# Gate and up products of two SwiGLU passes by seven products in place of eight, with the down products set between them

## The chip, the cores and the metric

One of the eight NeuronCores of a Trainium2 chip runs the whole program. The metric is the device time of one execution in microseconds (us), lower is better; the median of three runs stands for a kernel.

## The reference, cut to what matters

A decoder layer: a half-step SwiGLU FFN, two mixers side by side (attention and RWKV-7), and a second half-step FFN, over 1040 tokens (16 meta tokens and 1024) with d_model 1024 and d_ff 2816, all in float32.

```python
def swiglu(h, w_gate, w_up, w_down):
    return (jax.nn.silu(h @ w_gate) * (h @ w_up)) @ w_down
...
        n = rms_norm(h, ffn1_norm[l])
        h = h + 0.5 * swiglu(n, ffn1_w_gate[l], ffn1_w_up[l], ffn1_w_down[l])
...
        n = rms_norm(h, ffn2_norm[l])
        h = h + 0.5 * swiglu(n, ffn2_w_gate[l], ffn2_w_up[l], ffn2_w_down[l])
```

## The kernel before

**Tokens.** They go in two groups, A (528, in chunks of 256 and 272) and B (512). The order on TensorE is: ffn1 of A, projections of A, ffn1 of B, projections of B, the output product, ffn2 of A, ffn2 of B; the mixers' work is woven in between. Everything is kept with features on the 128 partitions and tokens along the free axis.

**Three matmuls per product.** A float32 operand is split into two fp32r tiles, a high part (ScalarE, `ACTIVATE`, tiles `whi`, `nh`, `ah`) and the rest (`wlo`, `nl`, `al`: a subtraction on VectorE, for most `al` on GpSimd). `mm3` issues high by high, high by low and low by high into one PSUM bank. Weights are split on the chip too: each 128x1024 block is loaded as `wraw` (512 KB, queue of SP), split into `whi` and `wlo`, and used once.

**One FFN (`ffn`).** The 22 tiles of 128 d_ff columns go in `PARTS` of 2, 4, 4, 4, 4 and 4 tiles. A gate tile is 8 contraction steps of `mm3` over the tokens (`pg`), then a sigmoid and a multiplication into `sl`; an up tile the same into `pu`, then a multiplication and the split into `ah`, `al`. After the tiles of a part (and the next part's first gate) come its down products (`pd`), four blocks `wraw` of 4 x 256 columns, each added into the residual `h` on VectorE. In group A each matmul has 256 or 272 columns; in group B's ffn2 it has 512, with 256 at its start and end.

**Other names.** `groupB(j)` (j = 0 to 3) normalizes and transposes 128 tokens of group B during A's ffn1 and writes them to DRAM (`nbd`, `xbd`); it uses the pool `xp`. `fin0` writes A's final output during the first tiles of B's ffn2, `final` writes B's at the end. `director` opens the mixers' pools after A's ffn1.

**What sets the order.** No order is written out for VectorE, ScalarE, GpSimd and SP: `Clock` records each instruction with a cost, keeps a modelled time for every engine (one shared `port` for GpSimd and those VectorE operations whose inputs all lie in SBUF), and puts the instructions out in the order in which they could start by it, urgent ones first. The result is one fixed program; on the chip each engine goes through its own list in order, waiting on semaphores. All instructions are issued from one recording line, so the profile shows the same line for all, and tiles tell them apart.

## Time and profile before

| what | us |
|---|---|
| runs of before: median of 3 (lowest, highest) | 2320.24 (2317.2, 2322.21) |
| the profiled execution: its time | 2319.39 |
| its span, first to last instruction | 2317.7 |
| PE (TensorE) busy in the span | 2275.8 (98%) |
| DVE (VectorE) busy | 1368.8 (59%) |
| ACT (ScalarE) busy | 965.5 (42%) |
| POOL (GpSimd) busy | 484.7 (21%) |

A row that lists instructions gives engine, operation, output tile <- input tiles and shapes; matmuls are pipelined, so that the time from one start to the next is what one costs, not its busy time. PEclk is the clock that TensorE was granted as a share of 2.4 GHz. A window row gives the window, its length, and for each engine its busy time with the number of instructions.

### The profile page before, as it was taken

The numbers are of one execution on the slowest core, as the hardware profiler recorded it, in microseconds if no ns is written. First come the engines' busy times: TensorE is split into PE (matmuls) and PEld (weight loads), VectorE is DVE, ScalarE is ACT, GpSimd is POOL, SyncE is SP. The second block draws the span as 40 slices with busy tenths as digits, with TensorE's granted clock in tenths as the row PEclk, the third lists the DMA queues.
The fourth block names the chain that finished last, engine by engine and source line by source line (L and its number), as shares of the span: only waits on it lengthen the run. The fifth ranks groups of instructions, "written<-read, shape, count | busy, mean of one in ns | idle before, by whom it ended". The sixth has DMA issues, their size and how long they took to land.

```text
span 2317.7 us, 40064 instructions
## 1 busy us (share of the span) xinstructions
PE 2275.8 (98%) x15931; PEld 1988.3 (86%) x15931; DVE 1368.8 (59%) x2325; ACT 965.5 (42%) x1871; POOL 484.7 (21%) x650
## 2 busy tenths in 40 slices
PE   7999999999999999999999989999999999999998
PEld 7999999999878788778878978887877898888888
DVE  5644444675776655676576877647777566433435
ACT  5422223543444434555434544445666333222222
POOL 0100011012042341441012324313544010000000
PEclk9999999999999999999999989999999999999999
DMA  4632322445652332422556433333222533333332
GB/s 129 191 117 88 91 89 91 139 139 138 213 138 81 93 92 83 119 90 74 159 142 195 137 96 98 91 89 119 82 77 69 154 99 124 91 100 91 91 100 82
DMA packets 412095, 259.59 MB, mean 112 GB/s; under 512 B 45060, under 2 KB 396500, under 8 KB 411908
## 3 DMA queue, kind: packets, MB, share of 16 engines
q1 hardware_dynamic: 411908, 257.04, 37.4%
q8 instruction: 125, 2.05, 0.4%
q14 instruction: 62, 0.51, 0.1%
HBM read 222.99 MB, written 33.99 MB: 111 GB/s over the span
## 4 chain that ended last, share of the span: by engine, by line
PE 93%; DVE 3%; DMA 1%; ACT 1%; issue 1%; POOL 0%; DVEq 0%; SPq 0%; ACTq 0%; POOLq 0%
PE pd L83 33%; PE pu L83 22%; PE pg L83 21%; PE pwo L83 3%; PE px L83 3%; PE po L83 2%; PE pz L83 2%; PE pat L83 2%; DVE wlo L83 1%; PE pG L83 1%; PE psw L83 0%; ACT whi L83 0%; DMA wraw<-in_ffn_w_gate_dram 0%; PE pp L83 0%; PE pxn L83 0%
## 5 line engine op out<-in xcount | busy, mean ns | idle before, releaser
L83 ACT ACTIVATE whi<-wraw 128x1024 fp32r<-128x1024 f32 (+1 forms) x348 | 366.7, 1054 | 528.2 <-PE pd L83 308.7
L83 DVE TENSOR_TENSOR wlo<-wraw,whi 128x1024 fp32r<-128x1024 f32 (+1 forms) x348 | 439.3, 1262 | 107.3 <-ACT whi L83 103.0
L83 PE MATMUL pd<-ah,whi 128*128 128x512 f32 (+2 forms) x944 | 326.1, 345 | 1.3 <-DVE h L83 1.2
L83 PE MATMUL pd<-al,whi 128*128 128x512 f32 (+2 forms) x944 | 318.4, 337 | 0.9 <-DVE al L83 0.8
L83 PE MATMUL pd<-ah,wlo 128*128 128x512 f32 (+2 forms) x944 | 318.9, 338 | 0.0
L83 POOL TENSOR_TENSOR al<-sl,ah 128x512 fp32r<-128x512 f32 (+1 forms) x83 | 124.5, 1500 | 925.4 <-ACT ah L83 925.2
L83 PE MATMUL pu<-nh,whi 128*128 128x512 f32 (+2 forms) x752 | 257.1, 342 | 0.0
L83 PE MATMUL pg<-nh,whi 128*128 128x512 f32 (+2 forms) x736 | 256.5, 348 | 0.0
L83 PE MATMUL pu<-nh,wlo 128*128 128x512 f32 (+2 forms) x752 | 248.0, 330 | 1.5 <-DVE wlo L83 1.5
L83 PE MATMUL pu<-nl,whi 128*128 128x512 f32 (+2 forms) x752 | 247.7, 329 | 0.0
L83 PE MATMUL pg<-nh,wlo 128*128 128x512 f32 (+2 forms) x736 | 246.6, 335 | 0.8 <-DVE wlo L83 0.8
L83 PE MATMUL pg<-nl,whi 128*128 128x512 f32 (+2 forms) x736 | 246.4, 335 | 0.2 <-DVE nl L83 0.2
L83 PE MATMUL pd<-nh,whi 128*128 128x256 f32 (+7 forms) x648 | 210.1, 324 | 0.9 <-DVE st L83 0.8
L83 PE MATMUL pd<-nh,wlo 128*128 128x256 f32 (+7 forms) x648 | 204.3, 315 | 0.4 <-DVE wlo L83 0.4
L83 PE MATMUL pd<-nl,whi 128*128 128x256 f32 (+7 forms) x648 | 204.1, 315 | 0.0
L83 PEld LDWEIGHTS pd<-ah,whi 128*128 128x128 f32 x944 | 177.5, 188 | 23.9 <-issue 2.6
L83 PEld LDWEIGHTS pd<-ah,wlo 128*128 128x128 f32 x944 | 177.7, 188 | 20.5
L83 PEld LDWEIGHTS pd<-al,whi 128*128 128x128 f32 x944 | 177.8, 188 | 19.6 <-DVE al L83 2.0
L83 DVE TENSOR_TENSOR sl<-pg,sl 128x512 f32<-128x512 f32 (+2 forms) x116 | 65.5, 564 | 199.8 <-ACT sl L83 199.5
L83 DVE SCALAR_TENSOR_TENSOR h<-pd,h 128x256 f32<-128x256 f32 (+1 forms) x200 | 107.9, 543 | 91.6 <-PE pd L83 90.4
L83 DVE TENSOR_TENSOR sl<-pu,sl 128x256 f32<-128x256 f32 (+2 forms) x119 | 65.9, 553 | 154.0 <-PE pu L83 153.5
L83 ACT ACTIVATE sl<-pg 128x512 f32<-128x512 f32 (+2 forms) x116 | 57.6, 497 | 234.5 <-PE pg L83 206.0
(275 smaller groups left out, 4826.0 us busy)
## 6 DMA issues: line engine op xcount, KB each, us to landing
wraw<-in_ffn_w_gate_dram SPq DMA_DIRECT2D x92, 512.0 KB
wraw<-in_ffn_w_up_dram SPq DMA_DIRECT2D x92, 512.0 KB
wraw<-in_ffn_w_down_dram SPq DMA_DIRECT2D x88, 512.0 KB
wraw<-in_w_in_dram SPq DMA_DIRECT2D x54, 512.0 KB
wraw<-in_w_out_dram SPq DMA_DIRECT2D x18, 512.0 KB
s<-rkvd SPq DMA_DIRECT2D x18, 256.0 KB
raw<-qkvd SPq DMA_DIRECT2D x16, 264.0 KB
raw<-qkvd SPq DMA_DIRECT2D x16, 256.0 KB
```

The lines of the kernel that those rows point to most:

```text
L83: self._c.trace(self._n, op, lambda: f(*a, **k), out, [x for x in args if isinstance(x, bass.AP)], k)
```

## The change

In the first FFN of group A and the last of group B, the d_ff tiles from 6 on (`QF`) are taken in pairs, for which gate (and up, but for the last pair) is computed as a *quad*: with the contraction halved, the two weight tiles of the pair as the other halving, and the tokens halved (w = 264 in A, 256 in B), the 2 x 2 block product is done with seven block products (Strassen in Winograd's form) instead of eight. A block product is 4 contraction steps of three matmuls over w columns.

- **Weight sums (`pair`).** Of the two raw tiles a1, a2 of a pair GpSimd forms s1, s2, s4, s3 (`qs`, 128x512 each), and five blocks are split into `qh`, `ql` (s1, s2, s4, s3 and half of a2); a1 is split whole into `whi`, `wlo`. The ring of `qh`, `ql` has seven places.
- **Token sums (`sums`).** Once per FFN, t1 to t4 are formed from the normalized tokens (`tt`) and split, four steps k.
- **Results (`quad`).** Partial results stay in PSUM; four copies to `sn` on ScalarE and four additions on VectorE put the two results together in SBUF tiles `cc` (2w wide). The sigmoid and both multiplications then read `cc` from SBUF.
- **Order (`quad_order`).** Down products of one part (d) stand between the quads of the next: d d d d g6 u6 g8 u8 | g10 d u10 d d g12 d u12 | g14 d u14 d d g16 d u16 | and so on; the last up pair is done plainly.
- **Memory.** The quads' pools take the place of `xp` and `wx` in A's ffn1, and of A's `h` and `n` and the pool `f2x` in B's ffn2, and open when `groupB` and `fin0` have let go of them. `groupB(j)` waits for block j - 2 instead of j - 1. The stage pool of the projections opens after the quads. B's `final` takes its output tiles from the ring `cc`.

```diff
+QF = 6
 PARTS = [(0, 2), (2, 6), (6, 10), (10, 14), (14, 18), (18, 22)]
...
+def quad_order():
+    for i, (f0, _) in enumerate(PARTS):
+        if f0 >= QF:
+            q = 0
+            for x in "ddddgu gu" if f0 == QF else "gdudd gdu":
+                if x == " ":
+                    f0 += 2
+                elif x == "d":
+                    yield x, PARTS[i - 1], q
+                    q += 1
+                else:
+                    yield x, None, f0
...
+class Fast:
+    def __init__(self, pools, w):
+        self.p, self.tp, self.q = pools
+        self.w, self.nq, self.nc, self.ns, self.k = w, 7, 7, 4, 0
+        self.t = {i: [self.tp.tile([P, 4, w], F32R, name="t%d%s" % (i, c)) for c in "hl"] for i in (1, 2, 3, 4)}
...
-            yield self.need(bank=(self.wp, "wr", 2))
-            self.wr.append((x, self.wraw(*x[:3])))
-            self.hold(self.wr[-1][1:])
+            raws = []
+            if isinstance(x[0], tuple):
+                for src, ring in zip(x[0], ((self.wp, "wr", 2), (self.fast.q, "wr2", 2))):
+                    yield self.need(bank=ring)
+                    raws.append(self.wraw(src, *x[1:3], ring))
+                    self.hold(raws[-1:])
+            else:
+                yield self.need(bank=(self.wp, "wr", 2))
+                raws.append(self.wraw(*x[:3]))
+                self.hold(raws)
+            self.wr.append((x, raws))
...
+        s1 = yield from part((a2[:, lo4], a2[:, hi4], ALU.add))
+        self.clock.ahead = True
+        self.split(w[0], w[1], a1)
+        out.append(([w[0][:, lo4], w[1][:, lo4]], ()))
+        out.append(([w[0][:, hi4], w[1][:, hi4]], w))
+        self.clock.ahead = False
+        s2 = yield from part((s1[1], a1[:, lo4], ALU.subtract))
+        halves(*s1)
+        a22 = yield from part()
+        self.split(a22[0], a22[1], a2[:, hi4])
+        self.clock.ahead = False
+        s4 = yield from part((a1[:, hi4], s2[1], ALU.subtract))
+        halves(*s2)
+        out.append((a22, a22))
+        s3 = yield from part((a1[:, lo4], a2[:, lo4], ALU.subtract))
+        halves(*s4)
+        halves(*s3)
...
-        half = [[self.fp.tile([P, 4, NA], F32R, tag="n%s%d" % (c, q), name="n%s%d" % (c, q)) for q in range(2)] for c in "hl"]
+        half = [[self.hp.tile([P, 4, NA], F32R, tag="n%s%d" % (c, q), name="n%s%d" % (c, q)) for q in range(2)] for c in "hl"]
...
+        def gates2(f):
+            yield lambda: self.fast and self.fast.k == 4
+            c = self.fast
+            x2 = yield from self.quad("pg", two(gw, f), bank)
+            for x in x2:
+                yield from self.room(c.p, ("cc", c.nc))
+                with self.urgent():
+                    sg = c.p.tile([P, 2 * c.w], F32, tag="cc", bufs=c.nc, name="sg")
+                    nc.scalar.activation(sg, x, AF.Sigmoid)
+                    nc.vector.tensor_tensor(out=x, in0=x, in1=sg, op=ALU.mult)
+            self.hold(x2)
+            return x2
+        def ups2(f, sls, acts):
+            x2 = yield from self.quad("pu", two(uw, f), bank)
+            for x, sl, a in zip(x2, sls, acts):
+                with self.urgent():
+                    nc.vector.tensor_tensor(out=x, in0=x, in1=sl, op=ALU.mult)
+                    self.split(a[0][:, 0:2 * self.fast.w], a[1][:, 0:2 * self.fast.w], x, nc.gpsimd)
...
+        for op, x, f in quad_order() if fast else ():
+            if op == "d":
+                yield from downs(x, f)
+            elif op == "g":
+                sls = yield from gates2(f)
             else:
-                for m in range(KT):
-                    if m % mw == 0:
-                        w = yield from dq(m // mw)
-                    for c in chunks:
-                        yield from down(*w, m, *c)
-                    if done and f1 == NFT:
-                        done(m)
+                act += [act_tiles(self.fast) if (f - QF) % 6 == 4 else act_tiles() for j in range(2)]
+                if f == NFT - 2:
+                    for j in range(2):
+                        w = yield from gu(uw, f + j)
+                        for e in edge:
+                            yield from up(w, sls[j][:, e[0]:e[1]], act[f + j], *e, True)
+                    self.flags["quads", nm] = True
+                else:
+                    yield from ups2(f, sls, act[f:])
+                self.drop(sls)
+        if fast:
+            yield from last(PARTS[-1])
...
+        for k in range(4):
+            yield self.need(*[b(j, q, i)[:, k] for j in range(2) for q in range(2) for i in range(2)])
+            x = []
+            for j in range(3):
+                yield from self.room(c.p, ("cc", c.nc))
+                t = c.p.tile([P, 2 * w], F32, tag="cc", bufs=c.nc, name="tt")
+                self.hold((t,))
+                x += [t[:, 0:w], t[:, w:]]
+            x11, x12, x22, x21, y = x[:5]
+            whole(V, x12, k, 0, 1)
+            whole(V, x11, k, 0, 0)
+            whole(G, x22, k, 1, 1)
+            whole(G, x21, k, 1, 0)
+            op(V, y, x12, x11, ALU.subtract)
+            self.split(c.t[1][0][:, k], c.t[1][1][:, k], y)
+            op(V, x11, x22, y, ALU.subtract)
+            self.split(c.t[2][0][:, k], c.t[2][1][:, k], x11)
+            op(V, x12, x22, x12, ALU.subtract)
+            self.split(c.t[3][0][:, k], c.t[3][1][:, k], x12)
+            op(G, x21, x21, x11, ALU.subtract)
+            self.split(c.t[4][0][:, k], c.t[4][1][:, k], x21)
+            self.drop(x[::2])
+            c.k = k + 1
...
+        def product(ps, x, first):
+            (wh, wl), gone = yield from get()
+            xh, xl = x
+            yield self.need(xh, xl)
+            for k in range(4):
+                mm = lambda l, r, start, stop: nc.tensor.matmul(ps, lhsT=l, rhs=r, start=start, stop=stop, skip_group_check=True)
+                mm(wh[:, k, :], xh[:, k], first and k == 0, False)
+                mm(wh[:, k, :], xl[:, k], False, False)
+                mm(wl[:, k, :], xh[:, k], False, k == 3)
+                yield
+            self.drop(gone)
+        def copy(ps):
+            yield from self.room(c.p, ("sn", c.ns))
+            with self.urgent():
+                t = c.p.tile([P, w], F32, tag="sn", bufs=c.ns, name="sn")
+                nc.scalar.activation(t, ps, AF.Copy)
+            return t
+        def add(j, i, ps, t):
+            with self.urgent():
+                nc.vector.tensor_tensor(out=out[j][:, i * w:i * w + w], in0=ps, in1=t, op=ALU.add)
+        x = c.x
+        px = yield from new("x")
+        yield from product(px, x["b11"], True)
+        p1 = yield from copy(px)
+        pw = yield from new("w")
+        yield from product(pw, x["b21"], True)
+        yield from cc()
+        add(0, 0, pw, p1)
+        py = yield from new("y")
+        yield from product(py, x["t1"], True)
+        p5 = yield from copy(py)
+        yield from product(px, x["t2"], False)
+        u2 = yield from copy(px)
+        pz = yield from new("z")
+        yield from product(pz, x["t4"], True)
+        yield from product(py, x["b22"], False)
+        add(0, 1, py, u2)
+        yield from product(px, x["t3"], False)
+        yield from cc()
+        add(1, 1, px, p5)
+        u3 = yield from copy(px)
+        add(1, 0, pz, u3)
+        return out
...
-            if j:
-                yield lambda: F.get(("xb", j - 1))
+            if j > 1:
+                yield lambda: F.get(("xb", j - 2))
...
+        def quads(nm, n, w, ready, old):
+            yield lambda: F.get(("part", nm)) and ready() and all(p_.quiet() for p_ in old())
+            for p_ in old():
+                p_.release()
+            c = [pool(nm + x, bufs=1, side="right") for x in "ptq"]
+            self.fast = Fast(c, w)
+            ck.spawn(self.sums(n(), self.fast), 12)
+            yield lambda: F.get(("quads", nm)) and all(p_.quiet() for p_ in c[1:])
+            for p_ in c[:0:-1]:
+                p_.release()
+            yield lambda: nm == "ffn1" and c[0].quiet() or F.get(("fin1", 0)) and F.get(("fin1", 1)) and c[0].quiet()
+            c[0].release()
+            self.fast = None
+            if nm == "ffn1":
+                self.stp = pool("stage", bufs=1)
+            F["fast1"] = True
...
-                    task(self.final(ssq["fin1", i], 1, f2["h"], slice(*chB[i]), bank, (f2["p"], ("mr", 4))), ("fin1", i))
-            yield from self.ffn("ffn2", f2["h"], f2["n"], ch, chB, bank, wait("n2_1"), hookE, True, wy=True)
+                    task(self.final(ssq["fin1", i], 1, f2["h"], slice(*chB[i]), bank, (self.fast.p, ("cc", self.fast.nc))), ("fin1", i))
+            yield from self.ffn("ffn2", f2["h"], f2["n"], ch, chB, bank, wait("n2_1"), hookE, True, wy=True, fast=True)
...
+        ck.spawn(quads("ffn1", lambda: n, NA // 2, lambda: F.get(("xb", 2)) and F.get(("xb", 3)), lambda: (xp, wx)), 5)
+        ck.spawn(quads("ffn2", lambda: f2["n"], NB // 2, lambda: F.get("fin0"), lambda: (f2["x"], self.hp)), 5)
```

**GpSimd, A's ffn1, before**: the splits `al` of d_ff tiles 5 to 7 and on, one per chunk.

```order
L83 TENSOR_TENSOR al<-sl,ah 128x272
L83 TENSOR_TENSOR al<-sl,ah 128x256
L83 TENSOR_TENSOR al<-sl,ah 128x272
L83 TENSOR_TENSOR al<-sl,ah 128x256
L83 TENSOR_TENSOR al<-sl,ah 128x272
```

**GpSimd, A's ffn1, after**, from the last token sums to the split of the first up quad: `tt` token sums, `qs` weight sums (s1 from `wraw` alone, s2 from `qs,wraw`, s4 from `wraw,qs`, s3 from `wraw` alone).

```order
L99 TENSOR_TENSOR tt<-tt 128x264
L99 TENSOR_TENSOR qs<-wraw 128x512
L99 TENSOR_TENSOR qs<-qs,wraw 128x512
L99 TENSOR_TENSOR qs<-wraw,qs 128x512
L99 TENSOR_TENSOR qs<-wraw 128x512 x2
L99 TENSOR_TENSOR qs<-qs,wraw 128x512
L99 TENSOR_TENSOR qs<-wraw,qs 128x512
L99 TENSOR_TENSOR qs<-wraw 128x512 x2
L99 TENSOR_TENSOR qs<-qs,wraw 128x512
L99 TENSOR_TENSOR qs<-wraw,qs 128x512
L99 TENSOR_TENSOR qs<-wraw 128x512 x2
L99 TENSOR_TENSOR al<-cc,ah 128x528 x2
```

Four weight sums per pair have come in; those of g6, u6 and g8 and the first of u8 stand ahead of the splits of u6.

**VectorE, A's ffn1, after**, from the last of the down products of d_ff tiles 2 to 5 (`h<-pd`) into the first quad g6 (`cc<-pg`): the weights' low parts stand between them.

```order
L99 SCALAR_TENSOR_TENSOR h<-pd,h 128x272
L99 TENSOR_TENSOR ql<-qs,qh 128x512
L99 TENSOR_TENSOR ql<-wraw,qh 128x512
L99 SCALAR_TENSOR_TENSOR h<-pd,h 128x256
L99 TENSOR_TENSOR ql<-qs,qh 128x512
L99 SCALAR_TENSOR_TENSOR h<-pd,h 128x272
L99 TENSOR_TENSOR ql<-qs,qh 128x512
L99 TENSOR_TENSOR wlo<-wraw,whi 128x1024
L99 TENSOR_TENSOR cc<-pg,sn 128x264
L99 TENSOR_TENSOR ql<-qs,qh 128x512 x2
L99 TENSOR_TENSOR ql<-wraw,qh 128x512
L99 TENSOR_TENSOR ql<-qs,qh 128x512
```

The same place before:

```order
L83 SCALAR_TENSOR_TENSOR h<-pd,h 128x272
L83 TENSOR_TENSOR wlo<-wraw,whi 128x1024
L83 SCALAR_TENSOR_TENSOR h<-pd,h 128x256
L83 SCALAR_TENSOR_TENSOR h<-pd,h 128x272
L83 SCALAR_TENSOR_TENSOR h<-pd,h 128x256
L83 SCALAR_TENSOR_TENSOR h<-pd,h 128x272
L83 TENSOR_TENSOR wlo<-wraw,whi 128x1024
```

Between the residual additions stood one split of 1024 columns for four of them; now five of 512 come in. The last low part of g6 stands behind the first addition of g6, and the whole split of u6's first tile (`wlo`) ahead of it.

**SP's queue, A's ffn1, after**, from the load of group B's last tokens to the last load ahead of the down blocks of tiles 2 to 5: `nbd`, `xbd` are writes of `groupB`, `wraw` weight loads.

```order
L99 DMA xt<-in_x_dram 128x1024
L99 DMA xbd<-rb 1024x1x128
L99 DMA wraw<-in_ffn_w_gate_dram 128x8x128
L99 DMA nbd<-bh 1024x1x128
L99 DMA nbd<-bl 1024x1x128
L99 DMA xbd<-rb 1024x1x128
L99 DMA wraw<-in_ffn_w_up_dram 128x8x128
L99 DMA nbd<-bh 1024x1x128
L99 DMA wraw<-in_ffn_w_gate_dram 128x8x128
L99 DMA nbd<-bl 1024x1x128
L99 DMA xbd<-rb 1024x1x128
L99 DMA wraw<-in_ffn_w_up_dram 128x8x128
```

The same place before:

```order
L83 DMA xt<-in_x_dram 128x1024
L83 DMA xbd<-rb 1024x1x128
L83 DMA wraw<-in_ffn_w_down_dram 128x4x256 x3
L83 DMA nbd<-bh 1024x1x128
L83 DMA nbd<-bl 1024x1x128
L83 DMA xbd<-rb 1024x1x128
L83 DMA wraw<-in_ffn_w_down_dram 128x4x256
```

The last block's writes stood among the down loads; now those of the last two blocks stand ahead of them, with two weight loads among them.

## Rows read from the trace of the kernel before

**Rows 1.** The page: busy time of each engine over the span (us, share, instructions), the granted clock in 40 equal slices, and the chain of work that ended last by engine.

```profile
PE 2275.8 (98%) x15931; PEld 1988.3 (86%) x15931; DVE 1368.8 (59%) x2325; ACT 965.5 (42%) x1871; POOL 484.7 (21%) x650
...
PEclk9999999999999999999999989999999999999999
...
PE 93%; DVE 3%; DMA 1%; ACT 1%; issue 1%; POOL 0%; DVEq 0%; SPq 0%; ACTq 0%; POOLq 0%
```

**Rows 2.** Windows of one full part of four d_ff tiles, in ffn1 of A and (two) in ffn2 of B: start:end and length, then busy time and instructions of PE, PE's weight load, DVE, ACT, POOL, then PEclk, DMA share, GB/s.

```profile
150.00:220.20 70.20, 70.20 (x579) 70.20 (x578) 28.92 (x46) 18.37 (x28) 6.68 (x6) 1.00 0.30 91
2002.00:2069.00 67.00, 67.00 (x290) 54.06 (x289) 26.30 (x29) 16.79 (x20) 5.23 (x3) 1.00 0.31 95
...
2069.00:2136.00 67.00, 67.00 (x290) 54.06 (x289) 26.30 (x29) 16.80 (x20) 5.23 (x3) 1.00 0.31 94
```

**Rows 3.** Timeline of TensorE in ffn1 of A, first matmul of four successive runs of 24 (gate and up of tile 5, chunk of 256 and of 272): start us, us, engine, line, operation, tiles, shapes.

```profile
102.17 0.28 PE L83 MATMUL pg<-nh,whi 128*128 128x256 f32 x1
...
104.99 0.29 PE L83 MATMUL pg<-nh,whi 128*128 128x272 f32 x1
...
108.01 0.28 PE L83 MATMUL pu<-nh,whi 128*128 128x256 f32 x1
...
110.82 0.29 PE L83 MATMUL pu<-nh,whi 128*128 128x272 f32 x1
```

**Rows 4.** Timeline of GpSimd, the same chunk's split in successive parts, in A and in B; in brackets the engine's idle time before and what ended it.

```profile
148.98 0.74 POOL L83 TENSOR_TENSOR al<-sl,ah 128x256 fp32r<-128x256 f32 x1 [43.73 <-ACT ah L83]
152.36 1.50 POOL L83 TENSOR_TENSOR al<-sl,ah 128x272 fp32r<-128x272 f32 x1 [2.65 <-ACT ah L83]
...
222.53 1.50 POOL L83 TENSOR_TENSOR al<-sl,ah 128x272 fp32r<-128x272 f32 x1 [2.65 <-ACT ah L83]
...
292.69 1.50 POOL L83 TENSOR_TENSOR al<-sl,ah 128x272 fp32r<-128x272 f32 x1 [2.65 <-ACT ah L83]
...
2048.72 1.74 POOL L83 TENSOR_TENSOR al<-sl,ah 128x512 fp32r<-128x512 f32 x1 [42.85 <-ACT ah L83]
...
2115.72 1.74 POOL L83 TENSOR_TENSOR al<-sl,ah 128x512 fp32r<-128x512 f32 x1 [42.85 <-ACT ah L83]
...
2182.72 1.74 POOL L83 TENSOR_TENSOR al<-sl,ah 128x512 fp32r<-128x512 f32 x1 [42.85 <-ACT ah L83]
```

**Rows 5.** Timelines around three meetings of `wlo` on VectorE and `al` on GpSimd (that of 2048.08 meets the `al` of 2048.72 in rows 4).

```profile
163.62 1.23 DVE L83 TENSOR_TENSOR wlo<-wraw,whi 128x1024 fp32r<-128x1024 f32 x1 [0.53 <-ACT whi L83]
163.98 1.49 POOL L83 TENSOR_TENSOR al<-sl,ah 128x272 fp32r<-128x272 f32 x1 [2.59 <-ACT ah L83]
...
2048.08 1.23 DVE L83 TENSOR_TENSOR wlo<-wraw,whi 128x1024 fp32r<-128x1024 f32 x1 [0.17 <-ACT whi L83]
...
794.09 1.27 POOL L83 TENSOR_TENSOR al<-sl,ah 128x512 fp32r<-128x512 f32 x1 [3.31 <-ACT ah L83]
794.11 2.34 DVE L83 TENSOR_TENSOR wlo<-wraw,whi 128x1024 fp32r<-128x1024 f32 x1
```

**Rows 6.** Groups of instructions over the span, shapes kept apart: count, busy us, mean ns of one, idle time before and what ended it.

```profile
L83 DVE TENSOR_TENSOR wlo<-wraw,whi 128x1024 fp32r<-128x1024 f32 x344 | 436.0, 1268 | 107.0 <-ACT whi L83 102.9 <-DMA rkvd<-st 1.9 <-DMA tw<-lod 0.5
L83 ACT ACTIVATE whi<-wraw 128x1024 fp32r<-128x1024 f32 x344 | 363.8, 1058 | 528.2 <-PE pd L83 308.7 <-PE pu L83 156.4 <-PE pwo L83 18.7
...
L83 ACT ACTIVATE sl<-pg 128x512 f32<-128x512 f32 x60 | 35.8, 597 | 138.2 <-PE pg L83 131.4 <-DMA wraw<-in_ffn_w_up_dram 4.2 <-POOL T L83 1.6
L83 ACT ACTIVATE ah<-sl 128x512 fp32r<-128x512 f32 x57 | 35.6, 625 | 5.1 <-DVE sl L83 5.0
L83 DVE TENSOR_TENSOR nacc<-nacc,nsq 128x256 f32<-128x256 f32 x56 | 24.1, 432 | 8.7 <-ACT nsq L83 8.1
L83 DVE SCALAR_TENSOR_TENSOR h<-pd,h 128x272 f32<-128x272 f32 x48 | 21.1, 440 | 23.7 <-PE pd L83 23.6
L83 DVE SCALAR_TENSOR_TENSOR acc<-acc,sw 128x512 f32<-128x512 f32 x24 | 16.4, 685 | 0.0
L83 ACT ACTIVATE ah<-sl 128x256 fp32r<-128x256 f32 x40 | 16.6, 414 | 53.2 <-DVE sl L83 53.2
```

**Rows 7.** Window from 88 to 137 us (gate and up of tiles 4 and 5 of A, gate of 6, and part of the down products of 2 to 5), columns as in rows 2.

```profile
88.00:137.00 49.00, 49.00 (x408) 49.00 (x407) 26.25 (x53) 17.68 (x29) 3.01 (x3) 1.00 0.54 160
```

**Rows 8.** Windows of 4 us in A's ffn1 with `groupB`'s transfers, columns as in rows 2, and SP's queue with the load of up of tile 5.

```profile
62.00:66.00 4.00, 4.00 (x36) 4.00 (x35) 2.86 (x6) 2.14 (x3) 0.00 (x0) 1.00 1.07 266
66.00:70.00 4.00, 4.00 (x35) 4.00 (x34) 2.80 (x9) 1.56 (x3) 0.00 (x0) 1.00 0.98 315
...
82.00:86.00 4.00, 4.00 (x36) 4.00 (x35) 1.76 (x3) 1.34 (x2) 0.00 (x0) 1.00 1.11 358
86.00:90.00 4.00, 4.00 (x34) 4.00 (x34) 1.15 (x5) 2.13 (x5) 0.84 (x2) 1.00 0.91 269
...
92.08 0.37 SPq L83 DMA_DIRECT2D wraw<-in_ffn_w_up_dram  x1
```

More of the change, by code (lines that the diff above doesn't have):

```diff
@@ L495, in splits @@
                 return
-            x, raw = self.wr[0]
+            x, raws = self.wr[0]
+            if len(raws) == 2:
+                self.wq.append((x, []))
+                yield from self.pair(raws, self.wq[-1][1])
+                self.drop(raws)
+                self.wr.pop(0)
+                continue
+            raw, = raws
             pool = self.wx if len(x) > 3 else self.wp
@@ L505, in hold, with wgetp, get @@
+    def wgetp(self, src):
+        self.drop(self.cur)
+        self.cur = ()
+        yield lambda: self.wq
+        x, parts = self.wq.pop(0)
+        assert [(a.name, a.offset) for a in x[0]] == [(a.name, a.offset) for a in src]
+        def get():
+            yield lambda: parts
+            w, gone = parts.pop(0)
+            yield self.need(*w)
+            return w, gone
+        return get
     def hold(self, tiles):
@@ new lines, in dq, with downs @@
+        def dq(part, q, keep=False):
+            f0, f1 = part
+            mw = KT // (f1 - f0)
+            return self.wget(dw[:, f0:f1, q * mw * P:(q + 1) * mw * P], f1 - f0, mw * P, keep)
+        def downs(part, q):
+            w = yield from dq(part, q)
+            mw = KT // (part[1] - part[0])
+            for m in range(q * mw, (q + 1) * mw):
+                for c in chunks:
+                    yield from down(*w, part, m, *c)
+                if done and part[1] == NFT:
+                    done(m)
@@ new lines, in last @@
+        def last(part):
+            late = []
+            mw = KT // (part[1] - part[0])
+            for m in range(KT):
+                if m % mw == 0:
+                    keep = wy and m >= KT // 2
+                    w = yield from dq(part, m // mw, keep)
+                for i, c in enumerate(edge[:1] if keep else edge):
+                    yield from down(*w, part, m, *c)
+                    hook(i, m)
+                if keep:
+                    late.append((m, w))
+            for m, w in late:
+                yield from down(*w, part, m, *edge[1])
+                hook(1, m)
+                if m % mw == mw - 1:
+                    self.drop(w)
@@ L783, in ffn @@
+        act = []
+        for part in PARTS:
+            f0, f1 = part
+            if fast and f0 >= QF:
+                break
             if f0 == 0 and first:
@@ new lines, in quad, with cc, new @@
+    def quad(self, name, src, bank):
+        nc, c = self.nc, self.fast
+        w = c.w
+        get = yield from self.wgetp(src)
+        out = []
+        def cc():
+            yield from self.room(c.p, ("cc", c.nc))
+            out.append(c.p.tile([P, 2 * w], F32, tag="cc", bufs=c.nc, name="cc"))
+        def new(nm):
+            yield self.need(bank=self.nextbank)
+            return bank(name)[:, 0:w]
+        def product(ps, x, first):
[14 more added lines that the diff above has]
+                nc.scalar.activation(t, ps, AF.Copy)
+            return t
+        def add(j, i, ps, t):
+            with self.urgent():
+                nc.vector.tensor_tensor(out=out[j][:, i * w:i * w + w], in0=ps, in1=t, op=ALU.add)
[22 more added lines that the diff above has]
+        return out
@@ L952, in ffn @@
                         yield gu("up", f)
+                if fast and f1 >= QF:
+                    continue
                 if f1 < NFT:
```

161 lines of the change are left out of this document (102 added, 59 removed).

## The prediction, made before the result was known

> **What bounds the kernel now.** I read the busy shares and the chain first [rows 1]: TensorE is busy 98% of the span and 93% of the chain that ends last; VectorE has 59%, GpSimd 21%. So a matmul less is time less, as long as nothing else becomes late. Then the stretch of one full part of four d_ff tiles in each of the two FFNs [rows 2]: TensorE is busy throughout, at a granted clock of 1.00 (2.4 GHz), VectorE some 40%, GpSimd under 10%, the DMA 0.3. Both engines that get new work have room on average; the question is the places where they have not.
>
> **What a matmul costs.** The split `al` of the same chunk comes every 70.17 us in A and every 67.00 us in B [rows 4]; a part holds 576 matmuls of 264 columns on average there (gate 192, up 192, down 192), 288 of 512 here: 121.8 ns and 232.6 ns each. From the first start of 24 to the next chunk's first [rows 3]: 2.82/24 = 117.5 ns for 256 columns, 3.02/24 = 125.8 ns for 272; their mean is 121.7, so 264 costs 121.8.
>
> **What the change removes.** A pair of tiles took 96 matmuls in A, 48 in B; a quad has 7 x 4 x 3 = 84. Fifteen quads per FFN (tiles 6 to 21: 8 gate, 7 up).
> - A: 15 x 12 x 121.8 ns = 21.9 us.
> - B: 15 x (48 x 232.6 - 84 x 117.5 ns = 1.295 us) = 19.4 us; two up tiles are now cut into 256 columns, 2 x (48 x 117.5 - 24 x 232.6) = 0.1 us back.
>
> Sum 41.2 us, if TensorE never waits. Of the two FFNs' middle parts each saves 5.8 us (A), 5.2 us (B).
>
> The Trainium skill, "TensorE: Matmul & The Clock Gate", Back-to-back issue gap, gives a gap of N/2.4 + 2.5 ns, that is 112.5, 109.2 and 215.8 ns for 264, 256 and 512 columns; by it the estimate would be 20.3 + 17.8 = 38.1 us. The rows here are 8% longer per matmul, and the measured ones stand in the sum.
>
> **What it adds, per quad.** Durations from [rows 6]: VectorE splits one 1024-wide block (1.23 alone [rows 5]) and five 512-wide (0.69, from `acc`, both inputs in SBUF) = 4.7 us, against 2.5 for two blocks before. Four additions from PSUM, 0.44 each (`h` 272) = 1.8. The two multiplications take 528 columns from SBUF, 0.71 each = 1.4, about what they took. ScalarE: 1.06 + 5 x 0.62 + 4 copies of 0.41 + 2 x 0.62 = 7.0 us of a quad's 10.2; hidden. GpSimd: four sums of 512 columns, and for an up quad two splits of 528.
>
> *One at a time.* GpSimd's operation and a VectorE operation with both inputs in SBUF do not run together: `al` (272) issued 0.36 us into a `wlo` takes 1.49 and ends 0.62 us after it, while 256 columns alone take 0.74 [rows 4, 5]; `al` (512) ends 1.15 us after `wlo`; and a `wlo` that starts 0.02 us behind an `al` of 1.27 us takes 2.34 instead of 1.23 [rows 5]. So I add both engines' such operations: 1.15 per sum of 512. That is what the Trainium skill says, "SBUF — State Buffer", Who interferes with whom: the port that GpSimd shares with VectorE is locked for the whole instruction, and a VectorE instruction with two SBUF inputs contends for it. The trace agrees. Without the rule nothing would be late and the sum would be 41.2; with it the terms below come in.
>
> Shared time per quad: weights 1.23 + 5 x 0.69 + 4 x 1.15 = 9.3; gate's multiplications 1.4; for an up quad 1.4 + 2 x 1.19 = 3.8. So 10.7 for a gate quad, 13.1 for an up quad, against 84 x 121.8 ns = 10.2 us of TensorE (9.9 in B). A down block between costs 1.2 of shared time against 5.85 (5.6 in B). Over a full part: 2 x 10.7 + 2 x 13.1 + 4 x 1.2 = 52.4 us against 64.3 (61.8 in B): hidden, if the order lets it be used. A quad's last block is needed 72/84 into it, and five of the seven places of `qh` come free while the quad before runs, so work can be nearly a quad late or early. Three places remain.
>
> 1. *The first five quads* have no down block between them. From g6's start to g10's last product TensorE needs 4 x 10.23 + 8.8 = 49.7 us (47.9 in B). Shared work due in it: four pairs' weights 37.1, the results of g6, u6, g8, u8 10.4, the last block of g6 0.7: 48.2. That fits if all 19 additions from PSUM (8.4 us) run beside GpSimd, and is up to 7 us (A), 9 us (B) late if none does. They use no shared port and GpSimd holds it half the time; I take 2 us in each FFN.
> 2. *A's run-up.* The token sums of A come after group B's blocks. Per step nine VectorE operations of 264 columns (0.43, `nacc` 256) and three of GpSimd (0.74): 15.5 + 8.9 us in all, behind them g6's weights, 4.7 + 4.6. In the 49 us that end near g6's start (88 to 137) VectorE is busy 26.3, GpSimd 3.0 [rows 7]; some 4 us of the former (`groupB`'s last block) move ahead. All in a row: 58.7 of 49; some 10 of these are PSUM reads that can overlap. So 0 to 10 us late; order and room being just enough, 2.5. In B the sums have the 79 us (340 matmuls) between `fin0` and g6: nothing.
> 3. *The loads in A.* Twelve writes of `groupB`, two `xt` and seven weight loads now follow each other, 21 x 0.52 MB. Busy stretches move 266 to 358 GB/s [rows 8], 1.5 to 2.0 us each: 32 to 42 us from 58 on, so 100 at worst. Up of tile 5, the last of them, is loaded at 92.08 and used at 108.01 [rows 3, 8]; 2.3 us go to its split. Nothing, at most 2 us.
>
> PSUM reuse adds nothing: between a copy and the next product into its bank lie 24 matmuls (2.9 us) against 0.41 us. The rest of the program keeps its order on TensorE from A's last down products to B's tile 4, with its few waits. The end (down products, `final`) is the same work.
>
> **Sum.** 2319.4 (the profiled execution; the median is 0.8 above it) - 41.2 + 2 + 2 + 2.5 = 2284.7: **2285 us**. Differences under 0.2% (4.6 us) can't be told from no change here.
>
> **Rivals.**
> - *No wait at all*: every addition and PSUM read overlaps. 2278 us. For it: 52.4 of 64.3 on average; against: places 1 and 2 leave 1 us in 49.
> - *VectorE with GpSimd becomes the bound*, in the middle parts too: the additions (7 us a part) and the residual's (4 x 4 x 0.44) never overlap GpSimd, 66.5 us a part instead of 64.3 in A, 65 instead of 61.8 in B. With places 1 and 2 at their ends too that gives back 3 x 2.2 + 7 + 10 in A and 3 x 3.2 + 9 in B, 42 us: 2320, no change. Half of it gives 2299; I take 2299 as its likely size. For it: each list is in order, so that an operation that waits for the port holds those behind it. Against: `wlo` and `al` already meet in each tile and TensorE does not wait.
> - *Slower: quads in lockstep with their weights.* If the seven places let a pair's weights be made only while the quad before runs, down blocks give no relief, and a quad takes its serial time, (10.7 + 13.1)/2 + 1.8 = 13.7 us, against 11.7 for a pair before (11.2 in B): 3.5 to 3.8 us over TensorE's per quad, 13 of them per FFN, 2278 + 95 = 2373 at its worst. It decides where quads average over 11.7 (A) and 11.2 us (B), 1.4 us of waiting each. For it: 5 of 7 places. Against: the order puts two quads' weights ahead of u6's splits on GpSimd.
> - *The change doesn't take effect*: excluded, the order shows 84 matmuls a pair.
>
> **How the numbers follow.** Forecast 0.5 (2281 to 2291), no wait 0.18, bound by VectorE and GpSimd 0.24 (2291 to 2320, a fifth of it within 0.2%), lockstep 0.08 (all slower). Faster 0.5 + 0.18 + 0.19 = 0.87, same 0.05, slower 0.08. The range takes in the first two with 2 us of spread below, and reaches halfway through the third: 2276 to 2305; left out are 0.08, about 0.09 of the third and 0.02 below.
>
> **What the profile will show.** Right: `al` or `cc` of full parts every 64.3 us in A, 62 in B; quads of 10.2 and 9.9 us; TensorE waits of 2 us or so for `ql` or `wlo` in g8 to g10, for `ql` in g6 of A; GpSimd 1.2 to 1.9 us per `qs`. Wrong: waits for `ql` at u10 and later (bound by VectorE and GpSimd), at every quad (lockstep), for `wraw` in tiles 3 to 5 of A (loads); or the first quad of A starting late after its down products by more than 10 us. A matmul of the quads that costs other than 117.5 or 121.8 ns would break the sum itself.

## The result, and the profile after

The changed kernel takes **2300.7 us** (median of four runs, 2299.8 to 2304.2) where the kernel before takes 2319.4 beside it: ratio 0.992, 95% interval 0.990 to 0.994. Four later runs beside others of before (2321.0) gave 2298.0 us, ratio 0.990 (0.989 to 0.992). It is faster by 19 to 23 us. Forecast were 2285 us in a range of 2276 to 2305: the direction and the range hold, but of the 35 us only some 60% came.

The page of the changed kernel, the lines that answer to those of before [rows 1]:

```profile
span 2298.3 us, 41595 instructions
...
PE 2244.2 (98%) x16339; PEld 1986.8 (86%) x16339; DVE 1579.3 (69%) x2605; ACT 1067.1 (46%) x2115; POOL 700.0 (30%) x786
...
PE 88%; DVE 6%; DMA 2%; ACT 2%; issue 1%; SPq 0%; DVEq 0%; ACTq 0%
```

TensorE's busy time fell by 31.6 us, the span only by 19.3. The chain says where to look: VectorE's share of it doubled from 3 to 6%. The windows of a full part in A and in B, of the first quads in A, and of A's run-up (columns as in [rows 2]):

```profile
226.36:290.58 64.22, 64.22 (x530) 64.22 (x529) 50.53 (x71) 29.60 (x52) 33.67 (x21) 1.00 0.36 99
2108.32:2170.96 62.64, 62.64 (x434) 58.31 (x432) 49.94 (x61) 29.65 (x52) 33.70 (x22) 1.00 0.36 102
144.38:198.51 54.13, 52.13 (x422) 51.28 (x421) 48.84 (x55) 28.10 (x54) 34.43 (x21) 1.00 0.34 94
...
88.00:137.00 49.00, 46.20 (x366) 45.99 (x365) 35.91 (x67) 17.97 (x35) 17.71 (x18) 0.97 0.42 122
```

A part in A takes 64.22 us, TensorE busy throughout, where 64.3 was worked out; one in B 62.64 where it was 61.8. The other losses are at the edges: TensorE idles 2.0 us in the first five quads of A (144.38 to 198.51) and 2.8 in the run-up (88 to 137).

So that no chance of the rest of the program is read as an effect, the span is cut at TensorE's instructions: from the first gate product to the first `nps` (A's first FFN), from there to B's first gate product on `n2B` (the middle, the same order in all kernels but for one swap of two matmuls in some), from there to the first `fss` of the tail (B's last FFN), and from there to the end (the rest). The 16 us ahead of the first gate product stand in no column. In us, for every profile taken:

```
                               A       middle     B       rest
before                       403.5    1510.4    370.6    16.6
after                        390.4    1513.9    359.9    18.1
after, second profile        391.7    1508.1    360.5    18.1
late sums                    391.4    1512.8    359.7    17.6
only A                       390.6    1516.7    370.6    16.6
only B                       405.8    1513.5    359.1    16.8
no weight sums               387.6    1512.7    355.2    16.6
weight sums on VectorE       388.7    1513.9    355.6    16.6
late, no weight sums         386.1    1513.2    355.2    16.6
late, all on VectorE         387.8    1511.9    355.6    16.6
wide rows                    388.9    1512.4    357.4    18.1
late, token sums on VectorE  387.9    1514.2    360.1    16.6
last quarter first           383.5    1513.8    352.8    16.6
```

A gained 12 to 13 us of the 21.9 worked out without waits, B 10 to 11 of 19.3. The middle ranges over 8.6 us without a rule: differences of single runs below that are not read from whole times here.

A's stretch holds a part of chance too. Its first 24 matmuls have the same order in all kernels and took 4.09 us in before (first two rows, start to start) and 5.00 in the changed kernel (last two); in its second profile it was 4.57, over all thirteen 3.98 to 5.41. The first of them start 0.21 us apart, until 18.3 us in before and 20.0 in the changed kernel, the others 0.12; no row shows why the one takes longer than the other. Without these 24 matmuls A gained 13.9 and 12.2 us.

```profile
16.52 0.58 PE L83 MATMUL pg<-nh,whi 128*128 128x256 f32 x1
...
20.61 0.28 PE L83 MATMUL pu<-nh,whi 128*128 128x256 f32 x1
```
```profile
16.01 0.58 PE L99 MATMUL pg<-nh,whi 128*128 128x256 f32 x1
...
21.01 0.28 PE L99 MATMUL pu<-nh,whi 128*128 128x256 f32 x1
```

**Where A lost.** The up product of d_ff tile 4 (256 columns) took 7.4 us where its 24 matmuls need 2.8. TensorE's starts, VectorE's first token sum, SP's issue it waited for, and windows around it:

```profile
98.63 0.28 PE L99 MATMUL pu<-nh,whi 128*128 128x256 f32 x1
...
106.05 0.28 PE L99 MATMUL pu<-nh,whi 128*128 128x272 f32 x1
```
```profile
97.57 1.12 DVE L99 TENSOR_TENSOR tt<-nh,nl 128x264 f32<-128x264 f32 x3 [8.06 <-DMA xbd<-rb]
98.61 0.43 DVE L99 TENSOR_TENSOR tt<-tt 128x264 f32<-128x264 f32 x1
98.95 0.43 DVE L99 TENSOR_TENSOR sl<-pu,sl 128x272 f32<-128x272 f32 x1
...
99.99 1.78 DVE L99 TENSOR_TENSOR wlo<-wraw,whi 128x1024 fp32r<-128x1024 f32 x1
```
```profile
91.30 1.66 SPq L99 DMA_DIRECT2D xbd<-rb  x1
```
```profile
98.00:102.00 4.00, 1.20 (x10) 0.99 (x9) 4.00 (x9) 1.38 (x4) 2.07 (x2) 0.99 0.00 0
102.00:106.00 4.00, 4.00 (x22) 4.00 (x23) 3.66 (x8) 1.51 (x4) 2.09 (x3) 0.59 0.44 131
```

The token sums' tiles lie in memory that `xp` gave back, and `xp`'s last write to DRAM, issued at 91.30, was still reading it. The planner had put the first `tt` at the head of VectorE's queue, where it stood 8.06 us; `sl` and the `wlo` of up of tile 4 stood behind it. TensorE was busy 1.20 of 4 us, and in the next 4 us its granted clock was 0.59: 4.6 us in all, of which the list of waits shows 2.8. In the second profile the same wait is 3.5 us, the clock in the 4 us after it 0.50, and the loss 6.2 us. The Trainium skill, "TensorE: Matmul & The Clock Gate", the paragraph on queue depths, calls ScalarE's and VectorE's queues strictly first in, first out; the 8.06 us are what that costs here.

**Where the first five quads lost.** VectorE, and GpSimd beside it, in g10 of A:

```profile
187.99 1.83 DVE L99 TENSOR_TENSOR ql<-qs,qh 128x512 fp32r<-128x512 f32 x1
189.74 0.42 DVE L99 TENSOR_TENSOR cc<-pg,sn 128x264 f32<-128x264 f32 x1
190.08 3.16 DVE L99 TENSOR_TENSOR ql<-qs,qh 128x512 fp32r<-128x512 f32 x2
```
```profile
187.47 3.53 POOL L99 TENSOR_TENSOR al<-cc,ah 128x528 fp32r<-128x528 f32 x2 [1.39 <-ACT ah L99]
190.96 1.73 POOL L99 TENSOR_TENSOR qs<-wraw 128x512 f32<-128x512 f32 x1
```

A `ql` of 0.68 us takes 1.83, three of them 5.0 us in which GpSimd splits `al` and sums. VectorE has no idle time before these rows: these `ql` stood in its queue behind lengthened operations, and did not wait for a sum of GpSimd to be finished. Four products of u8 and g10 took 0.3 to 1.2 us longer; added up, 3.1 us in A, and 4.5 in B (u8, g10, u10). After u10 no quad waits for weights.

### The profile page after: what moved, and what is told of

The parts are those of the page before. It is cut to its first block, busy times and chain, and to the rows that moved or that the text cites. A ratio compares the mean times of both kernels' runs of the same rounds, so it can differ in the third digit from the quotient of the medians.

```text
span 2298.3 us, 41595 instructions
## 1 busy us (share of the span) xinstructions
PE 2244.2 (98%) x16339; PEld 1986.8 (86%) x16339; DVE 1579.3 (69%) x2605; ACT 1067.1 (46%) x2115; POOL 700.0 (30%) x786
## 4 chain that ended last, share of the span: by engine, by line
PE 88%; DVE 6%; DMA 2%; ACT 2%; issue 1%; SPq 0%; DVEq 0%; ACTq 0%
PE pd L99 33%; PE pu L99 20%; PE pg L99 19%; PE pwo L99 3%; PE px L99 3%; PE po L99 2%; PE pz L99 2%; PE pat L99 2%; DVE wlo L99 2%; DVE ql L99 1%; PE pG L99 1%; ACT whi L99 1%; DVE cc L99 1%; PE psw L99 0%; SPq L99 0%
## 5 line engine op out<-in xcount | busy, mean ns | idle before, releaser
L99 PE MATMUL pu<-nh,whi 128*128 128x512 f32 (+3 forms) x584 | 210.1, 360 | 0.0
L99 PE MATMUL pu<-nh,wlo 128*128 128x512 f32 (+3 forms) x584 | 201.1, 344 | 4.1 <-DVE wlo L99 4.1
L99 PE MATMUL pg<-nh,whi 128*128 128x512 f32 (+3 forms) x544 | 200.9, 369 | 0.0
L99 PE MATMUL pu<-nl,whi 128*128 128x512 f32 (+3 forms) x584 | 200.5, 343 | 0.0
L99 POOL TENSOR_TENSOR al<-sl,ah 128x512 fp32r<-128x512 f32 (+2 forms) x47 | 77.8, 1655 | 389.5 <-ACT ah L99 384.2
L99 PE MATMUL pg<-nh,wlo 128*128 128x512 f32 (+3 forms) x544 | 191.4, 352 | 0.8 <-DVE wlo L99 0.8
L99 PE MATMUL pg<-nl,whi 128*128 128x512 f32 (+3 forms) x544 | 191.6, 352 | 0.2 <-DVE nl L99 0.2
L99 PEld LDWEIGHTS pd<-nh,whi 128*128 128x128 f32 (+2 forms) x648 | 120.2, 186 | 14.4 <-issue 3.2
L99 POOL TENSOR_TENSOR qs<-wraw 128x512 f32<-128x512 f32 x60 | 93.5, 1559 | 117.9 <-DVE ql L99 41.3
L99 PEld LDWEIGHTS pd<-nh,wlo 128*128 128x128 f32 (+2 forms) x648 | 120.3, 186 | 9.3 <-DVE wlo L99 0.6
```

Source lines behind the costliest of these rows:

```text
L99: self._c.trace(self._n, op, lambda: f(*a, **k), out, [x for x in args if isinstance(x, bass.AP)], k)
```

## The experiments

Ratios are to the kernel before. Four things had to be told apart: the two parts, the run-up's wait, the port, and what a matmul costs in B.

**Only A, only B.**

```diff
-        yield from ffn("ffn2", wx=True, fast=True)
+        yield from ffn("ffn2", wx=True)
...
-            yield from self.ffn("ffn2", ..., wy=True, fast=True)
+            yield from self.ffn("ffn2", ..., wy=True)
```

and the same for `ffn1` in the other kernel, whose A has the order of before.

> Only group A's first FFN goes by quads, group B's last FFN as before. If the two parts add up as their stretches in the trace say (A 13.5 us, B 10.7 us, 4.0 us lost between and 1.4 in the tail by chance of one execution), the time is about 2306 (2319.4 - 13.5). If what was lost in the middle (+4.0 us with the same order of instructions) belongs to what group A's quads leave behind, about 2309 to 2310, and the middle of this run is longer than that of before by 3 us or more; if it is chance, the middle is within 2 us of before.

> Only group B's last FFN goes by quads, group A's first FFN in the order of before. By the stretches of the trace the time is about 2309 (2319.4 - 10.7); by the sum of the prediction, with 19.4 less 2 us for this part, 2302. If matmuls of 256 columns there cost 120.0 ns instead of 117.5 (3.0 us) and the first five quads lose 4.5 us, as the trace of the changed kernel has it, it is 2308 to 2309. The middle (between group A's first FFN and B's last) should be that of before within 2 us, whatever the +4.0 is.

Measured: only A 2307.1 us, 0.994 (0.993 to 0.996); only B 2312.8, 0.996 (0.995 to 0.998). 13.8 and 8.1 us less, 21.9 together: the two parts add up, though only B is 4 us longer than the 2309 expected of it. The middle of only A was longer than that of before by 6.3 us, which by its text would speak for something that A's quads leave behind; but only B, with A's old order, has 3.0 more too, and the changed kernel's second profile 2.4 less than before. It is chance; that the middle would be within 2 us of before, as was expected of only B, did not hold either. What only B shows besides: A's stretch is 2.3 us longer though TensorE's order there is that of before. Of this 0.8 us is in the first 24 matmuls (4.86 us); 1.5 us comes on evenly over the rest of the stretch. What is known to have changed there is where the tiles lie (`h` and `n` moved to a pool of their own); that this is the cause was not tried by itself.

**Late sums.** The pools are handed over when the planner's clock says that the last user is done.

```diff
+            if nm == "ffn1":
+                yield max(0.0, max(ck.used(x) for p_ in old() for x in p_._names) - ck.pe) + 0.01
             for p_ in old():
                 p_.release()
```

> The changed kernel with one edit: the memory of group A's input tiles is handed to the token sums only when the planner's clock says that its last user is done, so the first token sum (tt) comes behind sl and wlo of tile 4 and 5 in VectorE's queue instead of ahead of them. Theory (the first token sum stood at the head of VectorE's in-order queue for 8.06 us until the transfer xbd<-rb had landed, and held up sl and wlo of tile 4): up of tile 4 takes about 3 us again instead of 7.4, group A's run-up is 4 to 5 us shorter, time about 2296. Rival 1 (the run-up is held up by the loads themselves, the DMA share being 0.93 to 1.09 there): up of tile 4 still waits for its weights, no change, about 2300.7. Rival 2 (VectorE and GpSimd simply have too much work in the run-up): the wait only moves to tile 5 or to the first quad g6, gain under 1.5 us, about 2299.5.

Measured: 2299.8 us, 0.991 (0.989 to 0.992); A's stretch 391.4 us, as before the edit. My theory half fell, and rival 2 came true: the wait at up of tile 4 went, and came back later, at the first down product of 272 columns:

```profile
118.75 0.43 DVE L99 TENSOR_TENSOR sl<-pu,sl 128x272 f32<-128x272 f32 x1
119.10 0.64 DVE L99 TENSOR_TENSOR t3l<-tt,t3h 128x264 fp32r<-128x264 f32 x1
119.67 1.76 DVE L99 TENSOR_TENSOR wlo<-wraw,whi 128x1024 fp32r<-128x1024 f32 x1
121.35 0.97 DVE L99 TENSOR_TENSOR al<-sl,ah 128x272 fp32r<-128x272 f32 x1
```
```profile
117.60 4.43 POOL L99 TENSOR_TENSOR tt<-nh,nl 128x264 f32<-128x264 f32 x4
```
```profile
122.00:126.00 4.00, 3.62 (x20) 3.62 (x21) 3.16 (x9) 0.00 (x0) 0.03 (x1) 0.69 0.43 135
```

GpSimd sums without a break from 117.60 to 122.03; beside it VectorE's `wlo` takes 1.76 us (1.23 alone) and `al` 0.97 (0.43). TensorE lost 4.4 us: 2.3 waiting, the rest at a granted clock of 0.69 after it. The transfer was one cause, and behind it stood another.

**No weight sums**, alone and with late sums. This part of the computation is left out, and the halves are split as they came (GpSimd makes four sums a quad; the expectation says five):

```diff
-                nc.gpsimd.tensor_tensor(out=raw, in0=x, in1=y, op=op)
                 self.clock.ahead = False
-                return t, raw
+                return t, x
```

> The changed kernel without GpSimd's five sums of weight halves a quad: the halves that were summed are split as they came (this part of the computation is left out; TensorE's work, ScalarE's and VectorE's splits are the same). Theory (the waits of the first five quads, 3.1 us in A and 4.5 us in B, come from GpSimd's sums, which hold VectorE's ql and GpSimd's al splits up and are held up by them): most of these waits vanish, the time is 5 to 8 us shorter, about 2294. Rival (they come from ScalarE and VectorE's splits and evacuations of the quads, or from the loads): the waits stay within 2 us of the same, about 2300.

> The kernel without weight sums (that part of the computation is left out) and with the token sums handed their memory late, as in the run before that did that alone. There the wait of 4.6 us at up of tile 4 went, and 4.4 us came back at the first down products of tile 5, where al waited behind token sums. Theory (the run-up is bound by VectorE and GpSimd together, token sums included; weight sums have no part in it since the first starts after 135 us): those 4.4 us stay without the weight sums, time about 2289 to 2290, as without late sums. Rival (what came back was due to weight splits or loads for the first quads): they go, about 2285.

Measured: 2289.7 us, 0.987 (0.985 to 0.988), and with late sums 2290.7, 0.987 (0.985 to 0.988). By whole times that is 8 to 11 us under the changed kernel, more than was expected. Alone, no wait of the first five quads is left in A, and none for weights in B; B's stretch is 4.7 us shorter. With late sums the wait of 2.3 us for `al` at the first down products is the same: weight sums have no part in the run-up.

**Weight sums on VectorE.**

```diff
-                nc.gpsimd.tensor_tensor(out=raw, in0=x, in1=y, op=op)
+                nc.vector.tensor_tensor(out=raw, in0=x, in1=y, op=op)
```

> The changed kernel with the weight sums qs of each quad moved from GpSimd to VectorE (the order on TensorE and of the loads is the same). Theory (GpSimd's and VectorE's operations with both operands in SBUF exclude each other, so a sum costs both engines its 1.2 to 2.15 us on GpSimd and would cost 0.6 on VectorE): the waits of the first five quads, 3.1 us in A and 4.5 in B, shrink by more than half, time 2294 to 2297. Rival (VectorE, with 69% of the span already, becomes the bound of the quads): waits for ql at every quad, slower than 2303.

Measured: 2292.9 us, 0.987 (0.985 to 0.989), better than forecast. TensorE's order is the same, VectorE does 120 operations more, and all waits but that of the run-up nearly vanish. TensorE's waits from 95 to 410 us and in B, here:

```profile
PE pu L99 <- DVE wlo L99: 3.1, 1, 3.1
...
PE fss L99 <- DVE nacc L99: 1.5, 1, 1.5
PE pg L99 <- DVE ql L99: 0.3, 1, 0.3
PE pd L99 <- DVE al L99: 0.3, 1, 0.3
```

and in the changed kernel:

```profile
PE pu L99 <- DVE wlo L99: 2.8, 1, 2.8
PE pg L99 <- DVE ql L99: 1.8, 2, 0.9
PE pu L99 <- DVE ql L99: 0.2, 1, 0.2
...
PE pg L99 <- DVE ql L99: 1.5, 1, 1.5
PE pu L99 <- DVE ql L99: 1.5, 4, 0.6
PE fss L99 <- DVE nacc L99: 1.5, 1, 1.5
PE pd L99 <- DVE al L99: 0.7, 2, 0.3
```

The waits for `ql`, 5.0 us in A and B together, fall to 0.3 while VectorE's list grows: it was not too long, it was held up by the other engine. The busy times say how much. The lines of the pages, without weight sums and with them on VectorE:

```profile
PE 2240.4 (98%) x16339; PEld 1986.4 (87%) x16339; DVE 1501.0 (66%) x2605; ACT 1068.8 (47%) x2115; POOL 496.0 (22%) x666
...
PE 2243.2 (98%) x16339; PEld 1988.9 (87%) x16339; DVE 1579.9 (69%) x2725; ACT 1072.0 (47%) x2115; POOL 497.7 (22%) x666
```

Without the 120 sums VectorE's 2605 operations take 1501.0 us; with the sums on GpSimd the same 2605 take 1579.3; with the sums on VectorE all 2725 take 1579.9. GpSimd's sums cost VectorE 78 us, as much as making them itself (79), and keep GpSimd busy some 200 us besides.

**Token sums on VectorE**, late; with weight sums on GpSimd, and with all on VectorE.

```diff
-        V, G = nc.vector, nc.gpsimd
+        V = G = nc.vector
```

> Late token sums, all token sums on VectorE, weight sums on GpSimd as in the changed kernel. Theory (GpSimd's token sums double VectorE's in the run-up): the wait of 4.4 us at the first down products, which late sums alone left, is under 1.5 us; the waits of the first five quads (3.1 and 4.5 us) stay, since GpSimd's weight sums stay; time 2295 to 2297. Rival (VectorE's own queue is too long in the run-up, whoever sums): 3 us or more of wait stay before the first quad, 2298 to 2301.

> The changed kernel with the token sums handed their memory late and all sums, of tokens and of weights, on VectorE. Theory (GpSimd's sums held VectorE's token sums and splits up: 0.43 us became 0.97 in the run-up): the wait for al at the first down products shrinks from 4.4 us to under 1.5, the waits of the first five quads by more than half; 2290 to 2293. Rival (VectorE's queue alone is too long in the run-up): a wait of 3 us or more stays at the first down products or at the first quad, 2294 to 2297.

Measured: 2298.3 us, 0.990 (0.989 to 0.992), and with all on VectorE 2291.9, 0.987 (0.986 to 0.989). The run-up itself runs without a wait in both, but a new one stands in g6, at the product of `t4`:

```profile
PE pg L99 <- ACT t4h L99: 2.5, 1, 2.5
```

(all on VectorE; 3.5 in the other), 5.7 us lost with its clock and the next two products. Both runs lie between theory and rival: the run-up is free, as the theories had it, but the loss stays, in the first quad, and the time of the first of the two is the rival's, that of the second the theory's. What is late is only the last quarter of the token sums: the planner rates them lower than weights, and VectorE had first split the weights of the next quad.

**Last quarter first**: the kernel that is late with all sums on VectorE, and besides the last quarter of the token sums urgent, and wide rows (below).

```diff
             x11, x12, x22, x21, y = x[:5]
+            self.clock.urg += k == 3
...
+            self.clock.urg -= k == 3
             self.drop(x[::2])
```

> The kernel with late token sums and all sums on VectorE, with two edits more: the last quarter of the token sums goes ahead of the weights in VectorE's queue, and the rows of n2B and the t tiles lie four columns further apart. Theory (in the kernel without these edits the first quad lost 5.7 us to t4 and t3 of the last quarter, which stood behind weight splits of the second quad; the wider rows are worth 2.4 us in B): the 5.7 us go but for 1 to 3 that come back as waits for weights of the second and third quad, time 2284 to 2287. Rival (VectorE has no room left there, what is put first only makes weights late): 4 us or more come back as waits for ql and wlo, 2288 to 2290.

Measured: **2286.1 us**, 0.984 (0.983 to 0.986), 35 us under before and 12 to 15 under the changed kernel: it beats both. In all of A from 95 us on TensorE waits once:

```profile
PE pg L99 <- DVE ql L99: 0.3, 1, 0.3
```

Its chain that ended last, 4% VectorE where the changed kernel has 6:

```profile
PE 92%; DVE 4%; DMA 1%; ACT 1%; issue 1%; POOL 0%; SPq 0%; DVEq 0%; ACTq 0%; POOLq 0%
```

A's stretch is 19.9 us under that of before. VectorE has all sums on its list and room for them: the rival, that what goes first only makes weights late, falls.

**Wide rows** alone. Every engine's order is the same; only the rows of the token tiles lie further apart, and tiles behind them in memory move with that.

```diff
-... self.tp.tile([P, 4, w], F32R, name="t%d%s" % (i, c)) ...
+... self.tp.tile([P, 4, w + 4], F32R, name="t%d%s" % (i, c))[:, :, 0:w] ...
-            half = [[f2b.tile([P, 4, NB], F32R, ...
+            half = [[f2b.tile([P, 4, NB + 4], F32R, ...
```

> The changed kernel with four columns more between the rows of the token tiles that B's matmuls read (n2B) and of the t tiles in both groups; the order of every engine is the same. Theory (a matmul of 256 columns costs 120.0 ns in B and 116.5 to 118.6 in A's tiles of 528 columns because of where the moving rows lie): matmuls of 256 columns in B fall to 117 to 118.5 ns, 2 to 3 us less, 2298. Rival (it is not the distance of the rows that makes the difference): 120 ns stays, time within 1 us of the same, 2300.7.

Measured: 2296.8 us, 0.990 (0.988 to 0.991); as a whole time not apart from the changed kernel's two, so the stretch has to speak: B's is 2.6 us shorter (3.1 against the second profile), and the quad g8 of B, 84 matmuls without a wait, goes from 10.08 us (120.0 ns each) to 9.91 (118.0). The first of the changed kernel, then of this one:

```profile
2046.73 0.28 PE L99 MATMUL pg<-n2Bh,whi 128*128 128x256 f32 x1
...
2056.81 0.28 PE L99 MATMUL pu<-n2Bh,whi 128*128 128x256 f32 x1
```
```profile
2042.74 0.28 PE L99 MATMUL pg<-n2Bh,whi 128*128 128x256 f32 x1
...
2052.65 0.28 PE L99 MATMUL pu<-n2Bh,whi 128*128 128x256 f32 x1
```

The price of 120.0 ns stood in the trace of before, where this FFN begins with 256 columns on the same tile (48 matmuls in 5.76 us):

```profile
1937.41 0.28 PE L83 MATMUL pg<-n2Bh,whi 128*128 128x256 f32 x1
...
1943.17 0.28 PE L83 MATMUL pg<-n2Bh,whi 128*128 128x256 f32 x1
```

That A's stretch is 1.5 us shorter than the changed kernel's does not speak for the rows: the first 24 matmuls took 3.98 us, 1.0 less, and up of tile 4 waited 2.7 us as it did there, but the granted clock did not fall after it (1.00 in the row below), so that the loss was 3.0 us instead of 4.6.

```profile
100.90:104.90 4.00, 4.00 (x34) 4.00 (x35) 3.66 (x8) 1.48 (x4) 2.12 (x3) 1.00 0.47 135
```

**The changed kernel again.**

> The changed kernel once more, for a second profile and more runs. Theory (the 4.0 us lost between group A's first FFN and the output projection, in a stretch whose order is that of before, belong to one execution; the nine profiles so far have 858.1 to 862.2 us there, without a rule): 858 to 862 us there again, time 2299 to 2302. Rival (they belong to the changed kernel): 861 us or more there in this profile too.

Measured: 2298.0 us, 1.0 below what was expected; its middle is 1508.1 us against 1513.9 in the first profile (from `nps` to the first `pwo` 857.0 against 862.2). The loss of 3.5 us in the first profile's middle belongs to that execution.

## Why the prediction was right, and where it was off

- *What the change removes in A*: right. 12 matmuls a pair at 121.8 ns; g6 takes 10.19 us for 84 (121.3 each), a part 64.22 of 64.3. With its waits gone (last quarter first) A gains 19.9 of 21.9 us, and 1.1 of the 2.0 left is in the first 24 matmuls (5.15 us against 4.09), ahead of all that was changed.
- *What it removes in B*: mis-sized. 256 columns were taken from A's tiles at 117.5 ns; on B's they cost 120.0. 15 x 84 x 2.5 ns = 3.2 us. The step that failed is taking a matmul's price from another tile with the same shape, though B's own tile had its price, 120.0, in the trace of before; the wide rows gave most of it back.
- *Place 1, the first five quads*: the mechanism was right, place and port too. 2 + 2 us was too little, 3.1 + 4.5 came, within the 7 and 9 named. I had let the additions from PSUM run beside GpSimd, and they did (0.42 us at 189.74 beside `al`); but a `ql` waits for each GpSimd operation before it, and in a queue in order all behind it wait as well. A weight sum was too cheap besides: 1.30 us where GpSimd's sums follow each other (row below), not 1.15, which is 2.4 us over the sixteen sums of this place.

```profile
136.41 1.30 POOL L99 TENSOR_TENSOR qs<-qs,wraw 128x512 f32<-128x512 f32 x1
```

- *Place 2, the run-up*: 2.5 us against 4.6 (6.2 in the second profile), within the 10 named (the terms of its list add up to 59.0 us, not 58.7), by a mechanism that I had missed, and which hid the one I had named. The first token sum waited for a transfer out of the memory it was to write; with that gone, VectorE's and GpSimd's sums cost nearly the same at a later place (late sums, 4.4 us). The second has two sources of its own: GpSimd's sums (0.97 us for an operation of 0.43), and with these on VectorE the order (the last quarter behind weights).
- *Place 3, the loads*: no product in the run-up waited for `wraw`, as said. But the transfers were not nothing: their end is what the first token sum waited for. I had asked which load is late, not whose memory is still being read.
- *The rivals.* Of VectorE with GpSimd as the bound of all parts there is nothing: the last wait is in u10 of B, 0.2 us. Lockstep didn't come: quads follow each other at TensorE's pace. "No wait" is what last quarter first nearly reached, 2286 us instead of 2278. Of the 8 us between, by the table, 2.0 are in A, 1.5 in B and 3.3 in the middle, which is within its chance; 1.3 lie between the span and the time.
- *The sum.* 2284.7 + 2.1 (run-up) + 3.6 (first quads) + 3.2 (256 columns) + 0.9 (first 24 matmuls) + 1.4 (the rest) + 3.5 (this execution's middle) = 2299.4; the profiled execution took 2300.6. In the second profile the run-up is 3.7, the 24 matmuls 0.5, the rest 1.5 and the middle -2.4: 2294.8, against 2297.2. Of the 1.2 and 2.4 us left, 0.9 and 1.5 are in B, and no run here shows where they come from. Why the rest is 1.4 us longer stays open too: the same instructions run there, and the span ends 4.1 us after the last issue of an output transfer, 2.7 in before and in most of the other kernels, all those with weight or token sums on VectorE among them.

## What to carry to other kernels

When a pool's memory is handed on, ask what still reads it, transfers above all, and what the first instruction on it stands in front of: an in-order engine passes the wait on to everything behind, and a new wait can hide a second one at the same place. GpSimd does not add its speed to VectorE's where both read two operands in SBUF: the weight sums moved from GpSimd to a VectorE that was 69% busy left it 69% busy and made the kernel 5 to 8 us faster. Before the price of a matmul goes into a sum a thousand times, take it from the tile that will be read, not from one of the same shape.

## What the runs showed of the hardware that was not expected

- Four columns (16 bytes) more between the rows of the moving tile change the distance of 256-column matmuls from 120.0 to 118.0 ns (g8 of B), in the same order of instructions. The Trainium skill, "TensorE: Matmul & The Clock Gate", Back-to-back issue gap, gives the isolated gap from the column count alone (N/2.4 + 2.5 ns), an estimate of 109.2 ns for 256; the quads here have 118.0 and 120.0.
- VectorE's operation of 264 columns takes 0.43 us alone and 0.97 beside GpSimd's sums, in the same stretch; with all sums on VectorE it is 0.42 to 0.43 in the run-up, but for one of 1.00 beside a split `al`. All of GpSimd's weight sums together took 78 us of VectorE's time. The Trainium skill, "SBUF — State Buffer", Who interferes with whom, has the exclusive lock; the traces agree, and show that the lock's price is paid by the queue behind.
- What a short wait of TensorE costs differs by execution. The wait at up of tile 4 was 2.6 to 3.5 us in six profiles and cost 3.0 to 6.2: after 2.8 us the granted clock of the next 4 us was 0.59 (at the lower of its two levels, 1.2 GHz, for most of it), after 3.5 it was 0.50, and after 2.7 in the wide rows' run it stayed at 1.00.
